# Three of five pieces of the inner layer norms: from VectorE to ScalarE and GpSimd

## The chip, the cores and the metric

The kernel runs on one core of a Trainium2 chip. The metric is the device time of one execution in microseconds (us). The core has these engines, each with an instruction queue of its own that is served in order: TensorE (PE, matmuls and transposes; PEld is its loading of weights), VectorE (DVE), ScalarE (ACT), GpSimd (POOL) and SyncE (SP), which here only issues DMA transfers. An engine waits at an instruction until the semaphores for it have come; whatever stands behind that instruction waits too.

## The reference

Two layers, each with a token mixer and a feed-forward part, both followed by a layer norm of the sum with the input. SEQ is 256, D_MODEL 2048, all in float32.

```python
for li in range(DEPTH):                              # DEPTH = 2
    proj = x @ w_in[li]
    ...                                              # three groups of heads
    mix = jnp.concatenate([ya, yb, yc], axis=-1) @ w_out[li]
    x = layer_norm(DEEPNORM_ALPHA * x + mix, ln1_g[li], ln1_b[li])
    ffn = (jax.nn.silu(x @ w_gate[li]) * (x @ w_up[li])) @ w_down[li]
    x = layer_norm(DEEPNORM_ALPHA * x + ffn, ln2_g[li], ln2_b[li])

def layer_norm(x, g, b, eps=1e-5):
    mu = xf.mean(-1, keepdims=True)
    var = jnp.mean(jnp.square(xf - mu), -1, keepdims=True)
    return (xf - mu) * lax.rsqrt(var + eps) * g + b
```

## The kernel before, in words

The 256 tokens are two tiles of 128 rows, t = 0 and 1; each lies in SBUF as `xs[t]`, 128 x 2048 (in rows of the order, `x0_75` and `x1_76`). All large products go through `run_groups`: a group is a block of up to 1024 output columns, and a step is one k (128 rows of the weights) for one t. The weights come in pairs of steps by DMA from SyncE's queue (`raw`, three buffers). `convert` splits each 128x1024 weight tile: ScalarE rounds it to `whi` (line 226), VectorE subtracts that from it to give `wlo` (line 227), and there are six buffers of each. A step then is six matmuls, two blocks of 512 columns in three passes on line 283: hi by hi, lo by hi, hi by lo. The left side is x transposed: TensorE transposes 128x128 blocks of x into a PSUM tile `aux` (line 306), and `split` writes the rounded half with ScalarE (`xth`, line 296) and the rest with VectorE (`xtl`, line 297). `pump(n)` asks for the conversions up to step n: it is called ahead of each step, so that the order in which the engines get their instructions is that of the program's text, sorted by a scheduler that also weighs priorities.

A layer norm stands between two groups. `res_evac` adds a finished block to x on VectorE (line 326) and takes its statistics (`bst`, line 330). `ln_finish` joins them (`mv`, `ve`) and GpSimd raises the variance to the power -1/2 (`rs`, line 342). `ln_apply` then norms x in five pieces, PIECES = (0,2), (2,4), (4,8), (8,12), (12,16) in blocks of 128 columns; a piece takes two operations of VectorE: (x - mean)*g on line 350 and *rs + b on line 353. They are here called p0 to p4. Between the two operations of t=1's first piece `between` pumps one weight conversion. Four norms are made: three inner ones (after out-projection 0 at 428 us of the span, after feed-forward 0 at 1152, after out-projection 1 at 1577) and the final one, which writes the output.

The first group behind an inner norm is skewed (`skew_in` 4): it takes k0 to k3 for t=0, then k0 to k3 for t=1, then from k4 on both t of each k. `xt_hooks` says where in this row the pieces are normed (`apply`) and transposed (`need`); `after(k, t)` runs behind each step. p2, the first far piece, is needed from k4 on, p3 from k8, p4 from k12. Behind the norm, VectorE holds the conversions of k4 and on.

Of the kernel before, what the change touches and what calls it, by code (L numbers as in the profile page):

```python
# [1 line left out]

# [1 line left out]

# [6 lines left out]
F32 = mybir.dt.float32  # L11
F32R = mybir.dt.float32r
BF16 = mybir.dt.bfloat16
AF = mybir.ActivationFunctionType
ALU = mybir.AluOpType
AX = mybir.AxisListType

P = 128
# [118 lines left out]
class Trunk:  # L137
# [79 lines left out]
    def convert(self, j):  # L217
        nc = self.nc
        w = self.steps[j][0]["width"]
        raw = self.raws[j // 2]  # L220
        src = raw[:, j % 2, 0:w]
        hi = self.wp.tile([P, 1024], F32R, name="whi", tag="whi", bufs=H_BUFS)
        lo = self.wp.tile([P, 1024], F32R, name="wlo", tag="wlo", bufs=H_BUFS)
        for o in range(0, w, w // 2 if j == 0 else w):
            s = slice(o, o + (w // 2 if j == 0 else w))
            nc.scalar.copy(out=hi[:, s], in_=src[:, s])  # L226
            nc.vector.tensor_tensor(out=lo[:, s], in0=src[:, s], in1=hi[:, s].bitcast(F32), op=ALU.subtract)  # L227
        self.whl[j] = (hi, lo)
        self.whl.pop(j - H_BUFS, None)
        if j % 2 == 1:  # L230
            del self.raws[j // 2]
            self.load_pair(j // 2 + RAW_BUFS)

    def pump(self, upto):

        while self.done < min(upto, len(self.steps)):
            self.convert(self.done)
            self.done += 1

    def run_groups(self, groups):  # L240

        nc = self.nc
        self.steps, self.pairs, self.raws, self.whl = [], [], {}, {}
        for g in groups:
            g["base"] = len(self.steps)
            for k in range(g["nk"]):
                self.steps.append((g, k))
                if k % 2 == 0:
                    self.pairs.append(g["src"](k))
        for p in range(RAW_BUFS):  # L250
            self.load_pair(p)
            for c in {1: (1,), 2: (2, 3)}.get(p, ()):
                for t in range(NT):
                    self.load_x(nc.sync, t, c)
        self.done = 0
        for g in groups:
            nk, nb, si, so = g["nk"], len(g["blocks"]), g.get("skew_in", 1), g.get("skew_out", 1)
            allb = tuple(range(nb))
            order = [(k, t, allb) for t in range(NT) for k in range(si)]
            order += [(k, t, allb) for k in range(si, nk - so) for t in range(NT)]  # L260
            order += [(k, t, (b,)) for t in range(NT) for b in allb for k in range(nk - so, nk)]
            banks = {}
            g["start"]()
            for (k, t, bs) in order:
                j = g["base"] + k
                if (k, t, bs[-1]) == (nk - 1, NT - 1, nb - 1) and "mid" in g:
                    g["mid"]()
                xh, xl = g["lhs"](k, t)
                ahead = AHEAD if k >= nk - so or k < si else FAR_AHEAD
                if k < si and t == 0 and si > 1:  # L270
                    self.pump(g["base"] + si)
                elif so > 1 and k == nk - 1 and t == NT - 1:
                    self.pump(j + SKEW + 1)
                else:
                    self.pump(j + ahead + 1)
                hi, lo = self.whl[j]
                for b in bs:
                    if (t, b) not in banks:
                        banks[t, b] = self.psum.tile([P, 512], F32, name="mm", tag="mm", bufs=MM_BUFS)
                for i, (lt, wt) in enumerate(((xh, hi), (xh, lo), (xl, hi))):  # L280
                    for b in bs:
                        o, w = g["blocks"][b]
                        nc.tensor.matmul(banks[t, b][:, 0:w], lt, wt[:, o:o + w],  # L283
                                         start=(k == 0 and i == 0), stop=(k == nk - 1 and i == 2))
                g["progress"] = k + 1
                if k == nk - 1:
                    for b in bs:
                        g["evac"](t, b, banks[t, b])
                if "after" in g and bs[-1] == nb - 1:
                    g["after"](k, t)  # L290
                if bs[-1] == nb - 1:
                    self.tasks.tick(g.get("budget", BUDGET) * g["width"] / 1024)


    def split(self, ps, hi, lo):
        self.nc.scalar.copy(out=hi, in_=ps)  # L296
        self.nc.vector.tensor_tensor(out=lo, in0=ps, in1=hi.bitcast(F32), op=ALU.subtract)  # L297

    def new_xt(self):
        return [self.xtp.tile([P, 4, SEQ], F32R, name=n, tag=n, bufs=4) for n in ("xth", "xtl")]  # L300
# [34 lines left out]
    def ln_finish(self, t, stats):  # L335
        nc = self.nc
        mv = self.small.tile([P, 2], F32, name="mv")
        nc.vector.bn_aggr(out=mv, in_=stats[t].rearrange("p c s -> p (c s)"))
        ve = self.small.tile([P, 1], F32, name="ve")
        nc.vector.tensor_scalar(out=ve, in0=mv[:, 1:2], scalar1=1e-5, scalar2=None, op0=ALU.add)  # L340
        rs = self.small.tile([P, 1], F32, name="rs")
        nc.gpsimd.tensor_tensor(out=rs, in0=ve, in1=self.mhalf[:, 0:1], op=ALU.pow)  # L342
        return mv, rs

    def ln_apply(self, t, k0, k1, mv, rs, between):
        nc = self.nc
        s = slice(k0 * P, k1 * P)
        z = self.xs[t][:, s]
        lg, lb = self.ln
        nc.vector.scalar_tensor_tensor(out=z, in0=z, scalar=mv[:, 0:1], in1=lg[:, s], op0=ALU.subtract, op1=ALU.mult)  # L350
        if between is not None:
            between()
        nc.vector.scalar_tensor_tensor(out=z, in0=z, scalar=rs, in1=lb[:, s], op0=ALU.mult, op1=ALU.add)  # L353

    def xt_hooks(self, mvrs):

        xt = self.xt = [None] * 4
        applied, done = set(), set()
        piece = lambda k: next(i for i, (a, b) in enumerate(PIECES) if a <= k < b)

        def apply(t, i, between=None):
            if (t, i) not in applied:
                applied.add((t, i))
                if mvrs is not None:
                    self.ln_apply(t, *PIECES[i], *mvrs[t], between)

        def need(t, i):
            if (t, i) not in done:
                done.add((t, i))
                apply(t, i)  # L370
                a, b = PIECES[i]
                if xt[a // 4] is None:
                    xt[a // 4] = self.new_xt()
                x = self.xs[t]
                self.tr_block([x[:, k * P:(k + 1) * P] for k in range(a, b)], xt[a // 4], a % 4, t)
                if i == 0:
                    apply(t, 1)

        def lhs(k, t):
            need(t, piece(k))  # L380
            hi, lo = xt[k // 4]
            s = slice(t * P, (t + 1) * P)
            return hi[:, k % 4, s], lo[:, k % 4, s]

        def after(k, t):
            if k == 0:
                need(t, 1)
            for i, (a, b) in enumerate(PIECES):
                if i >= 2 and (k, t) == (a - 4, 1):
                    apply(0, i)  # L390
                if i >= 2 and (k, t) == (a - 3, 1):
                    apply(1, i)
                if i >= 2 and (k, t) == (a - 2, 1):
                    need(0, i)
                if i >= 2 and (k, t) == (a - 1, 0):
                    need(1, i)
        return dict(lhs=lhs, after=after, apply=apply, need=need)

# [659 lines left out]
                groups[-1].update(skew_out=SKEW, mid=lambda: self.hooks["need"](0, 0))  # L1058
        return groups

    def ln_ready(self, t, stats):
        if t == 0:
            self.mvrs = {}
            self.hooks = self.xt_hooks(self.mvrs)
        self.mvrs[t] = self.ln_finish(t, stats)
        self.hooks["apply"](t, 0, (lambda: self.pump(self.done + 1)) if t else None)

    def ffn_groups(self, l):
        groups = []
        box = {}  # L1070
        for hf in range(2):
# [27 lines left out]
            for gi in range(2):  # L1099
# [15 lines left out]
                def evac(t, b, bank, hf=hf, gi=gi, last=last):  # L1115
                    self.res_evac(t, 2 * gi + b, bank, hf == 0, box["stats"] if hf else None)
                    if last and b == 1:
                        self.ln_ready(t, box["stats"])
                        if l == DEPTH - 1:
                            for i, (k0, k1) in enumerate(PIECES):  # L1120
                                self.hooks["apply"](t, i)
                                s = slice(k0 * P, k1 * P)
                                self.nc.sync.dma_start(out=self.out[0, t * P:(t + 1) * P, s], in_=self.xs[t][:, s])

# [53 lines left out]
```

## Time and profile before

| | |
|---|---|
| median of 3 runs | 2317.28 us (2317.12 to 2317.84) |
| the profiled execution, its own time | 2317.24 us |
| its span, first to last instruction | 2315.5 us |
| TensorE busy | 2296.5 us |
| VectorE busy | 1564.7 us |
| ScalarE busy | 1027.3 us |
| GpSimd busy | 36.7 us |
| granted TensorE clock, mean | 0.998 |

The span starts with the first instruction and ends with the last; 1.74 us of the execution's time lie around it. A busy time is the union of an engine's instructions. Where TensorE, the busiest, stands idle, time is lost; idle time of the others costs something only where it reaches TensorE.

### The profile page before, as it was taken

What the parts mean: (1) busy time and instruction counts of PE and PEld (TensorE: products, weight loads), DVE (VectorE), ACT (ScalarE), POOL (GpSimd) and SP (SyncE); (2) the same over time, 40 slices, a digit from 0 to 9 for tenths busy, and PEclk for the clock granted to TensorE, in tenths of its full rate; (3) what the DMA queues carried; (4) which work ended last, traced back from release to release, by engine and by line L of the source; (5) the groups of instructions that cost most, each with busy time, mean ns of one, the idle gap of its engine ahead of it and who ended that gap; (6) DMA issues with size and microseconds to landing.
All of it is one profiled execution on the core that took longest, in us unless ns stands there. A gap on an engine that the chain in (4) does not pass through costs nothing.

```text
span 2315.5 us, 27648 instructions
## 1 busy us (share of the span) xinstructions
PE 2296.5 (99%) x10474; PEld 1899.5 (82%) x10474; DVE 1564.7 (68%) x2596; ACT 1027.3 (44%) x1289; POOL 36.7 (2%) x78
## 2 busy tenths in 40 slices
PE   9999999999999999999999999999999999999997
PEld 7888888788888888888888888887888888888886
DVE  5885575767766447766578756657776764576765
ACT  5645554444444334444345465534444433444432
POOL 0000100000000000000000010000000000000000
PEclk9999999999999999999999999999999999999999
DMA  8555455555555555555556544565556555556553
GB/s 281 189 207 172 149 182 200 195 205 184 202 197 195 188 198 182 198 202 190 177 182 207 193 163 147 182 210 208 184 191 207 183 200 198 182 188 212 182 197 112
DMA packets 178934, 441.16 MB, mean 191 GB/s; under 512 B 15120, under 2 KB 22256, under 8 KB 177776
## 3 DMA queue, kind: packets, MB, share of 16 engines
q1 hardware_dynamic: 178656, 439.32, 55.7%
q8 instruction: 82, 1.34, 0.2%
q14 instruction: 52, 0.43, 0.1%
q10 hardware_dynamic: 144, 0.07, 0.0%
HBM read 437.25 MB, written 2.10 MB: 190 GB/s over the span
## 4 chain that ended last, share of the span: by engine, by line
PE 97%; DVE 2%; issue 1%; DMA 0%; ACT 0%; SPq 0%; POOLq 0%; POOL 0%
PE mm L283 94%; PE aux L306 1%; DVE x L353 0%; PE aux L573 0%; PE aux L668 0%; DVE x L350 0%; PE aux L435 0%; PE aux L758 0%; DVE bst L330 0%; DMA raw<-w_in 0%; PE aux L798 0%; PE aux L691 0%; PE aux L546 0%; DVE wlo L227 0%; ACT xth L296 0%
## 5 line engine op out<-in xcount | busy, mean ns | idle before, releaser
L227 DVE TENSOR_TENSOR wlo<-raw,whi 128x1024 fp32r<-128x1024 f32 (+2 forms) x817 | 983.1, 1212 | 659.1 <-ACT whi L226 653.6
L226 ACT CAST whi<-raw 128x1024 fp32r<-128x1024 f32 (+2 forms) x817 | 851.9, 1045 | 1138.5 <-PE mm L283 1100.6
L283 PE MATMUL mm<-whi,xth 128*128 128x512 f32 (+1 forms) x2560 | 808.6, 391 | 2.5 <-ACT xth L296 2.2
L283 PE MATMUL mm<-wlo,xth 128*128 128x512 f32 (+1 forms) x2560 | 798.4, 387 | 0.0
L283 PE MATMUL mm<-whi,xtl 128*128 128x512 f32 (+1 forms) x2560 | 796.9, 387 | 0.0
L283 PEld LDWEIGHTS mm<-wlo,xth 128*128 128x128 f32 x2560 | 476.6, 188 | 98.3 <-DVE wlo L227 0.2
L283 PEld LDWEIGHTS mm<-whi,xtl 128*128 128x128 f32 x2560 | 476.3, 188 | 98.6
L283 PEld LDWEIGHTS mm<-whi,xth 128*128 128x128 f32 x2560 | 469.9, 188 | 98.4 <-ACT xth L296 4.5
L283 PE MATMUL mm<-whi,gth 128*128 128x512 f32 x704 | 222.0, 389 | 0.0
L283 PE MATMUL mm<-whi,gtl 128*128 128x512 f32 x704 | 222.0, 389 | 0.0
L283 PE MATMUL mm<-wlo,gth 128*128 128x512 f32 x704 | 221.9, 389 | 0.0
L422 DVE STREAM_TRANSPOSE gtr<-sil 32x128 f32<-32x128 f32 x704 | 213.0, 303 | 11.2
L283 PEld LDWEIGHTS mm<-whi,gth 128*128 128x128 f32 x704 | 132.2, 188 | 27.6
L283 PEld LDWEIGHTS mm<-whi,gtl 128*128 128x128 f32 x704 | 132.2, 188 | 27.4
L283 PEld LDWEIGHTS mm<-wlo,gth 128*128 128x128 f32 x704 | 132.2, 188 | 27.3
L422 DVE STREAM_TRANSPOSE qk<-stg 32x128 f32<-32x128 f32 x256 | 77.4, 302 | 4.2
L296 ACT CAST xth<-aux 128x512 fp32r<-128x512 f32 (+1 forms) x58 | 29.1, 512 | 35.7 <-PE aux L306 29.9
L297 DVE TENSOR_TENSOR xtl<-aux,xth 128x512 fp32r<-128x512 f32 (+1 forms) x58 | 33.8, 594 | 6.8 <-ACT xth L296 6.8
L342 POOL TENSOR_TENSOR rs<-ve,mhalf 128x1 f32<-128x1 f32 x8 | 5.7, 718 | 1743.1 <-DVE ve L340 1743.1
L1140 DVE TENSOR_TENSOR gtl<-gtr,gth 128x512 fp32r<-128x512 f32 x44 | 29.9, 680 | 0.7
L1087 ACT ACTIVATE sil<-mm 128x512 f32<-128x512 f32 x44 | 25.9, 594 | 9.9 <-PE mm L283 9.9
L1090 DVE TENSOR_TENSOR sil<-mm,sil 128x512 f32<-128x512 f32 x44 | 28.2, 683 | 1.4 <-ACT sil L1087 1.4
(156 smaller groups left out, 635.6 us busy)
## 6 DMA issues: line engine op xcount, KB each, us to landing
raw<-w_gate SPq DMA_DIRECT2D x176, 512.0 KB, 3.7
raw<-w_up SPq DMA_DIRECT2D x176, 512.0 KB, 4.6
raw<-w_down SPq DMA_DIRECT2D x88, 1024.0 KB, 5.1
raw<-w_in SPq DMA_DIRECT2D x78, 1024.0 KB, 4.8
raw<-w_out SPq DMA_DIRECT2D x32, 1024.0 KB, 5.2
raw<-w_in SPq DMA_DIRECT2D x52, 512.0 KB, 4.0
raw<-w_in SPq DMA_DIRECT2D x16, 256.0 KB, 4.0
lng<-ln_g SPq DMA_DIRECT2D x4, 1024.0 KB, 7.7
```

The source lines that it names most:

```text
L226: nc.scalar.copy(out=hi[:, s], in_=src[:, s])
L227: nc.vector.tensor_tensor(out=lo[:, s], in0=src[:, s], in1=hi[:, s].bitcast(F32), op=ALU.subtract)
L283: nc.tensor.matmul(banks[t, b][:, 0:w], lt, wt[:, o:o + w], start=(k == 0 and i == 0), stop=(k == nk - 1 and i == 2))
L296: self.nc.scalar.copy(out=hi, in_=ps)
L297: self.nc.vector.tensor_tensor(out=lo, in0=ps, in1=hi.bitcast(F32), op=ALU.subtract)
L306: self.nc.tensor.transpose(out=ps[:, i * P:(i + 1) * P], in_=s, identity=self.ident)
L342: nc.gpsimd.tensor_tensor(out=rs, in0=ve, in1=self.mhalf[:, 0:1], op=ALU.pow)
L422: self.nc.vector.transpose(out=out[32 * j:32 * j + 32, 0:n, 32 * i:32 * i + 32], in_=in_[32 * i:32 * i + 32, 0:n, 32 * j:32 * j + 32])
L1087: nc.scalar.activation(out=box["s", t], in_=bank, func=AF.Silu)
L1090: nc.vector.tensor_tensor(out=g, in0=bank, in1=g, op=ALU.mult)
L1140: nc.vector.tensor_tensor(out=lo, in0=gt, in1=hi.bitcast(F32), op=ALU.subtract)
```

## The change

In the three inner norms the pieces p2 to p4 go to other engines. `ln_finish` has two more operations of GpSimd for nm = -mean*rs. `ln_apply_far` makes a piece by one ScalarE activation (x*rs + nm, in place) and two GpSimd operations of 128x512, times g and plus b. `ln_apply` keeps p0 and p1 on VectorE without anything between its two operations; one conversion is asked for behind the second. The hooks move: p2 of t=0 is asked for in `ln_ready`, p2 of t=1 behind the first step of t=1, p3 and p4 of both t six and five steps ahead of their use and behind the last far piece. While the skew lasts, VectorE's half of a conversion is tied behind the last `xtl` (`fence`). The transposes of p2 of t=1 move from behind k3 of t=0, that is from ahead of all of t=1's steps, to behind k3 of t=1; those of p3 and p4 of t=1 stand directly behind those of t=0. The final norm keeps all pieces on VectorE (`far=False`).

```diff
@@ convert
-            nc.vector.tensor_tensor(out=lo[:, s], in0=src[:, s], in1=hi[:, s].bitcast(F32), op=ALU.subtract)
+            with ExitStack() as st:
+                if self.fence is not None:
+                    st.enter_context(self.tc.issue_after(self.fence))
+                nc.vector.tensor_tensor(out=lo[:, s], in0=src[:, s], in1=hi[:, s].bitcast(F32), op=ALU.subtract)
...
-    def pump(self, upto):
+    def pump(self, upto, behind=None):
+        self.fence = behind
...
-                    self.pump(j + ahead + 1)
+                    self.pump(j + ahead + 1, self.last_lo if 1 < si and k < si else None)
@@ ln_finish
+        nm = self.small.tile([P, 1], F32, name="nm")
+        nc.gpsimd.tensor_tensor(out=nm, in0=mv[:, 0:1], in1=rs, op=ALU.mult)
+        nc.gpsimd.tensor_scalar(out=nm, in0=nm, scalar1=-1.0, scalar2=0.0, op0=ALU.mult, op1=ALU.add)
...
+    def ln_apply_far(self, t, k0, k1, mv, rs, nm):
+        nc = self.nc
+        s = slice(k0 * P, k1 * P)
+        z = self.xs[t][:, s]
+        lg, lb = self.ln
+        nc.scalar.activation(out=z, in_=z, func=AF.Identity, bias=nm, scale=rs)
+        nc.gpsimd.tensor_tensor(out=z, in0=z, in1=lg[:, s], op=ALU.mult)
+        self.last_far = nc.gpsimd.tensor_tensor(out=z, in0=z, in1=lb[:, s], op=ALU.add).ins
...
-        if between is not None:
-            between()
-        nc.vector.scalar_tensor_tensor(out=z, in0=z, scalar=rs, in1=lb[:, s], op0=ALU.mult, op1=ALU.add)
+        last = nc.vector.scalar_tensor_tensor(out=z, in0=z, scalar=rs, in1=lb[:, s], op0=ALU.mult, op1=ALU.add).ins
+        if behind is not None:
+            behind(last)
@@ xt_hooks, after(k, t)
             if k == 0:
+                if mvrs is not None and t:
+                    with self.tc.issue_after(self.last_hi):
+                        apply(1, 2)
                 need(t, 1)
             for i, (a, b) in enumerate(PIECES):
-                if i >= 2 and (k, t) == (a - 4, 1):
-                    apply(0, i)
-                if i >= 2 and (k, t) == (a - 3, 1):
-                    apply(1, i)
-                if i >= 2 and (k, t) == (a - 2, 1):
+                if i < 2:
+                    continue
+                near = i == 2
+                skewed = near and mvrs is not None
+                if mvrs is not None and i > 2:
+                    for u in range(NT):
+                        if (k, t) == (a - 6 + u, 1):
+                            with self.tc.issue_after(self.last_far), self.tc.issue_after(self.last_hi):
+                                apply(u, i)
+                if (k, t) == (a - 2, 1):
                     need(0, i)
-                if i >= 2 and (k, t) == (a - 1, 0):
+                if (k, t) == ((a - 1, 1) if skewed else (a - 1, 0) if near else (a - 2, 1)):
                     need(1, i)
@@ ln_ready
-        self.hooks["apply"](t, 0, (lambda: self.pump(self.done + 1)) if t else None)
+        self.hooks["apply"](t, 0, (lambda ins: self.pump(self.done + 1, ins)) if t else None)
+        if not final and t == 0:
+            self.hooks["apply"](t, 2)
```

Where instructions stand is shown at the first inner norm. `whi_3629` before and `whi_3635` after is the conversion of k2; the next is k3, then k4, k5 and so on. First ScalarE, from the conversion of k2 on, before:

```order
L226 CAST whi_3629<-raw_3520 128x1024
L226 CAST whi_3665<-raw_3520 128x1024
L296 CAST xth_3644<-aux_3646 128x2x128
L226 CAST whi_3746<-raw_3555 128x1024
L226 CAST whi_3763<-raw_3555 128x1024
L296 CAST xth_3644<-aux_3684 128x2x128
```

and after:

```order
L227 CAST whi_3635<-raw_3520 128x1024
L361 ACTIVATE x0_75<-x0_75,nm_3621,rs_3619 128x512
L227 CAST whi_3675<-raw_3520 128x1024
L303 CAST xth_3650<-aux_3652 128x2x128
L227 CAST whi_3745<-raw_3555 128x1024
L227 CAST whi_3767<-raw_3555 128x1024
L303 CAST xth_3650<-aux_3693 128x2x128
L303 CAST xth_3650<-aux_3716 128x2x128
```

The activation of t=0's p2 now stands ahead of the conversion of k3 and of the first `xth` (p0 of t=0, out of `aux_3652`), the one of t=1 behind the `xth` of t=1's p0 (`aux_3716`).

Next VectorE behind the norm's last operation on t=1's p1. Before, with the `xtl` of t=1's p2 (`aux_3711`), p0 (`aux_3718`) and p1 (`aux_3733`), the conversions of k4 to k8 (`wlo_3747` to `wlo_3788`), and the `xtl` of t=0's p2 (`aux_3756`):

```order
L297 TENSOR_TENSOR xtl_3710<-aux_3711,xth_3709 128x4x128
L297 TENSOR_TENSOR xtl_3645<-aux_3718,xth_3644 128x2x128
L227 TENSOR_TENSOR wlo_3747<-raw_3555,whi_3746 128x1024
L297 TENSOR_TENSOR xtl_3645<-aux_3733,xth_3644 128x2x128
L227 TENSOR_TENSOR wlo_3764<-raw_3555,whi_3763 128x1024
L227 TENSOR_TENSOR wlo_3777<-raw_3596,whi_3776 128x1024
L227 TENSOR_TENSOR wlo_3781<-raw_3596,whi_3780 128x1024
L227 TENSOR_TENSOR wlo_3788<-raw_3669,whi_3787 128x1024
L297 TENSOR_TENSOR xtl_3710<-aux_3756,xth_3709 128x4x128
```

After, from the joined statistics of t=1 on; `wlo_3676` is the conversion of k3, `aux_3716` and `aux_3734` are p0 and p1 of t=1, `aux_3757` p2 of t=0 and `aux_3780` p2 of t=1:

```order
L345 BN_AGGR mv_3664<-bst_2937 128x2
L347 TENSOR_SCALAR ve_3666<-mv_3664 128x1
L370 SCALAR_TENSOR_TENSOR x1_76<-x1_76,mv_3664,lng_3349 128x256 x2
L371 SCALAR_TENSOR_TENSOR x1_76<-x1_76,rs_3668,lnb_3350 128x256
L231 TENSOR_TENSOR wlo_3676<-raw_3520,whi_3675 128x1024
L371 SCALAR_TENSOR_TENSOR x1_76<-x1_76,rs_3668,lnb_3350 128x256
L304 TENSOR_TENSOR xtl_3651<-aux_3716,xth_3650 128x2x128
L304 TENSOR_TENSOR xtl_3651<-aux_3734,xth_3650 128x2x128
L231 TENSOR_TENSOR wlo_3746<-raw_3555,whi_3745 128x1024
L304 TENSOR_TENSOR xtl_3756<-aux_3757,xth_3755 128x4x128
L231 TENSOR_TENSOR wlo_3768<-raw_3555,whi_3767 128x1024
L231 TENSOR_TENSOR wlo_3791<-raw_3596,whi_3790 128x1024
L304 TENSOR_TENSOR xtl_3756<-aux_3780,xth_3755 128x4x128
```

The conversion of k3, which before stood ahead of the last statistics of t=1, now stands between the second operations of t=1's near pieces. The `xtl` of p2 of t=0 moves from behind the conversion of k8 to behind that of k4; that of t=1, which stood ahead of all of them, moves behind those of k5 and k6 (`wlo_3768`, `wlo_3791`).

Last GpSimd after; before, its queue held only the two `rs` here:

```order
L352 TENSOR_SCALAR nm_3621<-nm_3621 128x1
L362 TENSOR_TENSOR x0_75<-x0_75,lng_3349 128x512
L363 TENSOR_TENSOR x0_75<-x0_75,lnb_3350 128x512
L349 TENSOR_TENSOR rs_3668<-ve_3666,mhalf_90 128x1
L351 TENSOR_TENSOR nm_3670<-mv_3664,rs_3668 128x1
L352 TENSOR_SCALAR nm_3670<-nm_3670 128x1
L362 TENSOR_TENSOR x1_76<-x1_76,lng_3349 128x512
L363 TENSOR_TENSOR x1_76<-x1_76,lnb_3350 128x512
L362 TENSOR_TENSOR x0_75<-x0_75,lng_3349 128x512
L363 TENSOR_TENSOR x0_75<-x0_75,lnb_3350 128x512
L362 TENSOR_TENSOR x1_76<-x1_76,lng_3349 128x512
L363 TENSOR_TENSOR x1_76<-x1_76,lnb_3350 128x512
```

GpSimd's `rs` of t=1 stands behind both operations on p2 of t=0; the far pieces stand in one row behind it, each waiting for its activation. SyncE's load of the next norm's g (line 318, its buffer being the g of this one) now waits for the last of these products instead of for VectorE; it keeps its place among the weight loads.

## Rows read from the trace of the kernel before

**Rows 1.** The page: busy time, share of the span and instructions of each engine.

```profile
PE 2296.5 (99%) x10474; PEld 1899.5 (82%) x10474; DVE 1564.7 (68%) x2596; ACT 1027.3 (44%) x1289; POOL 36.7 (2%) x78
```

**Rows 2.** What TensorE waited for: total us, times, longest us.

```profile
PE mm L283 <- ACT xth L296: 2.2, 3, 0.7
PE aux L306 <- DVE x L353: 1.7, 3, 0.6
```

**Rows 3.** Timeline of TensorE, norm one: start, duration, line, what, count, idle before.

```profile
430.66 0.65 PE L283 MATMUL mm<-whi,xth 128*128 128x512 f32 x2
...
437.13 0.84 PE L306 MATMUL aux<-cst_sb,x 128*128 128x128 f32 x6 [0.57 <-DVE x L353]
438.71 0.73 PE L283 MATMUL mm<-whi,xth 128*128 128x512 f32 x2 [0.73 <-ACT xth L296]
...
445.00 0.68 PE L283 MATMUL mm<-whi,xth 128*128 128x512 f32 x2
...
447.81 0.62 PE L283 MATMUL mm<-whi,xth 128*128 128x512 f32 x2
...
449.17 0.62 PE L283 MATMUL mm<-whi,xth 128*128 128x512 f32 x2
```

**Rows 4.** Timeline of VectorE in the same stretch, same columns.

```profile
431.90 1.22 DVE L227 TENSOR_TENSOR wlo<-raw,whi 128x1024 fp32r<-128x1024 f32 x1
...
433.96 0.25 DVE L338 BATCH_NORM_AGGREGATE mv<-bst 128x2 f32<-128x24 f32 x1
...
435.85 1.14 DVE L353 SCALAR_TENSOR_TENSOR x<-x,rs,lnb 128x256 f32<-128x256 f32 x2
...
437.30 1.14 DVE L353 SCALAR_TENSOR_TENSOR x<-x,rs,lnb 128x512 f32<-128x512 f32 x2
```

**Rows 5.** Timeline of ScalarE in the same stretch, same columns.

```profile
429.00 1.05 ACT L226 CAST whi<-raw 128x1024 fp32r<-128x1024 f32 x1 [5.75 <-PE mm L283]
430.16 0.37 ACT L296 CAST xth<-aux 128x256 fp32r<-128x256 f32 x1
```

**Rows 6.** Timeline of GpSimd in the same stretch, same columns.

```profile
428.26 0.72 POOL L342 TENSOR_TENSOR rs<-ve,mhalf 128x1 f32<-128x1 f32 x1 [146.45 <-DVE ve L340]
434.95 0.72 POOL L342 TENSOR_TENSOR rs<-ve,mhalf 128x1 f32<-128x1 f32 x1 [5.97 <-DVE ve L340]
```

**Rows 7.** A group of GpSimd by shape: count, busy us, mean ns, idle before.

```profile
L626 POOL TENSOR_TENSOR rrs<-rrs,dm 128x4 f32<-128x4 f32 x4 | 0.8, 202 | 0.3
```

**Rows 8.** One line each: ns minimum, median, maximum, first and last start, forms.

```profile
L652 POOL TENSOR_TENSOR mixc<-mixc,nrm x16: 592/599/1585, 232.5 to 1386.2; 128x192 f32<-128x192 f32 x16
L350 DVE SCALAR_TENSOR_TENSOR x<-x,mv,lng x40: 469/742/751, 428.1 to 2310.2; 128x512 f32<-128x512 f32 x24, 128x256 f32<-128x256 f32 x16
```

**Rows 9.** The page's group of the activations of 128x512.

```profile
L1087 ACT ACTIVATE sil<-mm 128x512 f32<-128x512 f32 x44 | 25.9, 594 | 9.9 <-PE mm L283 9.9
```

**Rows 10.** Timeline of GpSimd at 1384, two of its products.

```profile
1383.58 2.14 POOL L652 TENSOR_TENSOR mixc<-mixc,nrm 128x192 f32<-128x192 f32 x2
```

**Rows 11.** Timeline of VectorE in the same stretch.

```profile
1384.02 1.25 DVE L227 TENSOR_TENSOR wlo<-raw,whi 128x1024 fp32r<-128x1024 f32 x1 [5.33 <-ACT whi L226]
```

**Rows 12.** Timeline of VectorE at 203.

```profile
203.00 1.22 DVE L227 TENSOR_TENSOR wlo<-raw,whi 128x1024 fp32r<-128x1024 f32 x1 [1.84 <-ACT whi L226]
```

**Rows 13.** Timeline of GpSimd: the small scalings at 203 and 238.

```profile
203.75 0.52 POOL L623 TENSOR_SCALAR rve<-ssa 128x2 f32<-128x2 f32 x1 [5.51 <-ACT work L803]
...
238.06 0.19 POOL L623 TENSOR_SCALAR rve<-ssa 128x2 f32<-128x2 f32 x1
```

**Rows 14.** The second half: us, busy us of each engine (x instructions), clock, DMA, GB/s.

```profile
445.00:468.00 23.00, 23.00 (x110) 19.09 (x110) 17.87 (x21) 10.44 (x12) 0.00 (x0) 1.00 0.91 327
```

**Rows 15.** SyncE's DMA queue around the second half.

```profile
454.44 0.34 SPq L318 DMA_DIRECT2D lng<-ln_g  x1
459.45 0.37 SPq L214 DMA_DIRECT2D raw<-w_gate  x1
```

**Rows 16.** The page's DMA issues: count, KB each, median us to landing.

```profile
raw<-w_gate SPq DMA_DIRECT2D x176, 512.0 KB, 3.7
```

More of the change, by code (lines that the diff above doesn't have):

```diff
@@ L1 @@
 import math
+from contextlib import ExitStack
 import numpy as np
@@ L238, in pump @@
             self.done += 1
+        self.fence = None
     def run_groups(self, groups):
@@ L295, in split @@
     def split(self, ps, hi, lo):
-        self.nc.scalar.copy(out=hi, in_=ps)
-        self.nc.vector.tensor_tensor(out=lo, in0=ps, in1=hi.bitcast(F32), op=ALU.subtract)
+        self.last_hi = self.nc.scalar.copy(out=hi, in_=ps).ins
+        self.last_lo = self.nc.vector.tensor_tensor(out=lo, in0=ps, in1=hi.bitcast(F32), op=ALU.subtract).ins
     def new_xt(self):
@@ L342, in ln_finish, with ln_apply @@
         nc.gpsimd.tensor_tensor(out=rs, in0=ve, in1=self.mhalf[:, 0:1], op=ALU.pow)
-        return mv, rs
-    def ln_apply(self, t, k0, k1, mv, rs, between):
+        nm = self.small.tile([P, 1], F32, name="nm")
+        nc.gpsimd.tensor_tensor(out=nm, in0=mv[:, 0:1], in1=rs, op=ALU.mult)
+        nc.gpsimd.tensor_scalar(out=nm, in0=nm, scalar1=-1.0, scalar2=0.0, op0=ALU.mult, op1=ALU.add)
+        return mv, rs, nm
+    def ln_apply_far(self, t, k0, k1, mv, rs, nm):
[6 more added lines that the diff above has]
+        self.last_far = nc.gpsimd.tensor_tensor(out=z, in0=z, in1=lb[:, s], op=ALU.add).ins
+    def ln_apply(self, t, k0, k1, mv, rs, nm, behind):
         nc = self.nc
@@ L359, in xt_hooks, with apply @@
         piece = lambda k: next(i for i, (a, b) in enumerate(PIECES) if a <= k < b)
-        def apply(t, i, between=None):
+        def apply(t, i, behind=None, far=None):
             if (t, i) not in applied:
                 applied.add((t, i))
-                if mvrs is not None:
-                    self.ln_apply(t, *PIECES[i], *mvrs[t], between)
+                if mvrs is not None and (i >= 2 if far is None else far):
+                    self.ln_apply_far(t, *PIECES[i], *mvrs[t])
+                elif mvrs is not None:
+                    self.ln_apply(t, *PIECES[i], *mvrs[t], behind)
         def need(t, i):
@@ L1059, in out_groups, with ln_ready @@
         return groups
-    def ln_ready(self, t, stats):
+    def ln_ready(self, t, stats, final=False):
         if t == 0:
@@ L1117, in evac @@
                     if last and b == 1:
-                        self.ln_ready(t, box["stats"])
+                        self.ln_ready(t, box["stats"], l == DEPTH - 1)
                         if l == DEPTH - 1:
                             for i, (k0, k1) in enumerate(PIECES):
-                                self.hooks["apply"](t, i)
+                                self.hooks["apply"](t, i, far=False)
                                 s = slice(k0 * P, k1 * P)
```

## The prediction

> **What bounds the kernel now.** I read the page's busy times first: TensorE is busy 99% of the span [rows 1], so only time in which it stands idle, or gets more to do, counts. The view of its waits comes second: two waits belong to the inner norms, three times each, 2.2 us for ScalarE's `xth` and 1.7 us for VectorE's line 353 [rows 2]. The timeline of norm one shows where. TensorE is through with t=0's four steps at 436.56 and waits 0.57 us for the second operation on p2 of t=1, whose transposes stand ahead of all of t=1's steps; the `xth` behind these six transposes costs another 0.73 us [rows 3]. VectorE's timeline has the cause: a conversion of 1.22 us at 431.90 stands in front of the joined statistics at 433.96, and at 435.85 and 437.30 operations on far pieces stand between those that t=1's first step needs [rows 4]. The other norms have the same pair. From 445.00 to 468.00 TensorE never stops, with VectorE busy 17.87 of 23 us [rows 14]. So the change can win at most the 3.9 us of these waits, 0.17% of the time; 0.2% is about what this measurement tells from no change.
>
> **What goes and what comes.** Each inner norm loses 12 VectorE operations of 0.742 us [rows 8], 8.9 us, and gains 6 activations, 12 GpSimd products of 128x512 and 4 tiny GpSimd operations. Where VectorE's 8.9 us stood beside TensorE's work they bring nothing; the two waits are all that they cost.
>
> An activation of 128x512 takes 0.594 us [rows 9]; the one shown reads PSUM, mine reads SBUF, and I take 0.59. A GpSimd product of 128x512 is in no row. From below: 128x4 takes 0.202 us [rows 7] and 128x192 0.592 at least [rows 8], which is 2.07 ns an element, hence 0.592 + 320 x 0.00207 = 1.26 us. From above, in proportion: 0.592 x 512/192 = 1.58. I take 1.3, because the small row shows that a part of the time does not grow with the size. Both operations on a piece are then 2.6 to 3.2 us instead of 1.5 on VectorE.
>
> The Trainium skill (GPSIMD Engine Reference, the table that reconciles measured numbers) gives 4497 ns for 2048 elements against 2293 on VectorE; an estimate by a quarter would be 1.12 us, a little under my lower end, and the sum below would hardly move. No row here has that size.
>
> *Start of the skew, norm one.* GpSimd ends `rs` at 428.98 [rows 6]; two tiny operations of 0.2 us each and the handing over let the activation of t=0's p2 start at about 429.65. It stands ahead of k3's conversion on ScalarE, which ran at 429.00, and that stands ahead of the first `xth`, which ran at 430.16 [rows 5]. Now: activation to 430.2, conversion 430.1 to 431.1, `xth` at 431.08. So TensorE's first step of t=0 starts at 431.58 instead of 430.66 [rows 3]: 0.92 us later.
>
> *End of t=0.* TensorE's work up to 436.56 took 5.90 us; it now has to wait for VectorE's half of k3's conversion, which has moved behind t=1's first second operation. With `xth` late the `xtl` in front of the joined statistics is late too, and 433.96 becomes 434.15; `rs` of t=1 then runs 434.65 to 435.37 (0.72 as before), the norm's second operation on p0 starts at 435.55, and the conversion runs from 435.94 to 437.16. TensorE can use it at 437.25, some 0.5 to 0.7 us after it wants it, and with two passes of 0.45 us (a third of the step of 1.36, 447.81 to 449.17) t=1 begins at 438.16. Before it began at 438.71 [rows 3].
>
> *t=1.* From there to k4 it took 6.29 us [rows 3]; four transposes of p2 come in, about 0.3 us, so k4 starts near 444.75 instead of 445.00. Up to here the two waits, 1.3 us, have shrunk to a gain of 0.25 us, since ScalarE's place and k3's conversion take their room: three norms 0.75 us.
>
> *From k4 on.* VectorE now has the `xtl` of t=1's p2 behind the conversions of k5 and k6. By my schedule these run at 444.91 and 446.04, and the `xtl` ends at 447.9; TensorE wants it at 447.9. There is no slack. In this moment, about 444.85, GpSimd begins with p3 of t=0. Does a GpSimd product hold up a VectorE conversion? The trace has the other direction: a scaling of 0.19 us by itself at 238.06 [rows 13] takes 0.52 at 203.75, begun under a conversion from 203.00 to 204.22 [rows 12], and ends just behind it; six such overlaps of six look so. At 1383.58 two products take 2.14 us [rows 10] instead of twice 0.592 [rows 8], with a conversion from 1384.02 [rows 11]. That conversion began before the product under way was through, and took 1.25 instead of 1.22; so from this one row the price for VectorE lies anywhere between nothing and the rest of a product.
>
> The bounds: nothing, if VectorE is never held; one product of 1.2 to 1.35 us, if the first conversion gets in ahead of GpSimd and the product between the two conversions holds the second; two products, 2.5 us, if GpSimd gets in first. I take the middle, 1.2, as both begin within 0.06 us of each other, and the row at 1384 shows a conversion little delayed when it starts upon a running product. Per norm: -0.25 + 1.2 = +0.95.
>
> The Trainium skill (SBUF — State Buffer, who interferes with whom) says that a VectorE instruction with two SBUF inputs and a GpSimd instruction that reads SBUF exclude each other, and that the second to start is fully blocked. The six overlaps agree in one direction; the 1.25 us at 1384.02 neither shows nor refutes the other. By this rule the price would be the 1.2 to 2.5 us just bounded.
>
> **The sum**, against the profiled run's own 2317.24 (0.04 under the median): 2317.24 + 3 x 0.95 = 2320.1, said as 2320.0.
>
> **The rivals.**
>
> *A: both waits simply go.* If ScalarE's and VectorE's new places cost nothing (nm earlier than I think, k3's conversion in time) and GpSimd holds nobody up: 2317.24 - 3.9 = 2313.3. Against it: the order on ScalarE and VectorE is fixed, and the two delays follow from durations in rows. Chance 0.10, and in about half of it some more small gaps around the transposes go too and it passes 0.2%.
>
> *C: no hold-up of VectorE.* Start and skew as worked out, nothing behind: 2317.24 - 0.75 = 2316.5. For it: the conversion at 1384.02. Chance 0.27.
>
> *B, the forecast:* 2320 to 2324, the upper end with 2.5 us in each norm. Chance 0.42, about two thirds of it below 2321.9.
>
> *D, the slower side: GpSimd starves and p3 comes late.* Four products on p3 (5.1 to 6.3 us) must lie between 444.85 and 452.7, where their transposes are wanted. VectorE has six conversions to make there, some 7 us of work at up to 1.22 each. If it goes from one to the next without letting GpSimd in, the products begin only at about 451.8 and end at 457 or later, over 4 us late; with 4.8 as a price: 2316.5 + 3 x 4.8 = 2330.9. It decides from the point at which fewer than three products get in before 450. Against it: VectorE must wait for ScalarE's half of most conversions, since these wait for a buffer that TensorE frees. Chance 0.16.
>
> *E: the weight loads come late.* The load of the next norm's g, at 454.44 before, now waits for GpSimd's last product with g, at about 462 to 464, and the weight load of 459.45 [rows 15] stands behind it. That load has two pairs of steps, 2 x 5.44 us, less its landing of 3.7 [rows 16] and some 0.9 for the issues, before its first conversion: 6.3 us of slack. It costs from 465.7 on, one for one, in the two norms ahead of a feed-forward part; with the last product at 468, 2316.5 + 2 x 2.3 = 2321.1. Chance 0.05.
>
> **How the numbers follow.** Faster by over 0.2% (under 2312.65) is half of A, 0.06 with rounding up. Slower by over 0.2% (over 2321.9) is a third of B, D and a little of E: 0.35. The rest, 0.59, is within 0.2%. The range leaves out half of A below and most of D above: 2313 to 2329. Cases of both signs inside the 0.2% make up the most; the likeliest one's own range is 2320 to 2324.
>
> **What would show it.** ScalarE's first `xth` at about 431.1 and TensorE's first step at 431.6; TensorE waiting for `wlo` of line 231 in k3 of t=0, and no longer for line 371 (353 before); GpSimd's products taking 1.2 to 1.6 us alone, and some with the length of a conversion on top; conversions of more than 1.3 us on VectorE, if it is held; TensorE's wait for `xtl` of line 304 at about 448. The prediction is wrong if conversions stay at 1.22 us while products run (then C), if the waits for lines 313 or 304 behind p3 are of several us (D), or if the products are not within 1.2 to 1.6.

## The result and the profile after

The changed kernel takes 2334.34 us (median of 4 runs, 2334.24 to 2335.13) against 2317.31 of before: a ratio of 1.0075 with a 95% interval of 1.0063 to 1.0087, slower by 17.0 us. The forecast was 2320.0, at most 2329. The range missed, and the profile says at once that something stands in it that the forecast never spoke of.

TensorE's waits, as total, times and longest, are what the forecast talked about, and they are small:

```profile
PE mm L289 <- ACT xth L303: 2.7, 3, 0.9
PE mm L289 <- DVE xtl L304: 2.0, 3, 0.7
PE mm L289 <- DVE wlo L231: 1.6, 3, 0.6
...
PE aux L313 <- DVE x L371: 0.7, 3, 0.3
```

7.0 us where there were 3.9 [rows 2]. But the page has TensorE busy 14.7 us longer [rows 1], with the same 10474 instructions:

```profile
PE 2311.2 (99%) x10474; PEld 1900.3 (81%) x10474; DVE 1563.3 (67%) x2560; ACT 1037.1 (44%) x1307; POOL 107.7 (5%) x130
...
L289 PE MATMUL mm<-whi,gth 128*128 128x512 f32 x704 | 226.2, 395 | 0.0
L289 PE MATMUL mm<-wlo,gth 128*128 128x512 f32 x704 | 226.0, 395 | 0.0
L289 PE MATMUL mm<-whi,gtl 128*128 128x512 f32 x704 | 225.9, 395 | 0.0
```

These three groups are the down-projections, whose left side is `gth` or `gtl`. No line of the change touches them. Before, their rows on the page were:

```profile
L283 PE MATMUL mm<-whi,gth 128*128 128x512 f32 x704 | 222.0, 389 | 0.0
L283 PE MATMUL mm<-whi,gtl 128*128 128x512 f32 x704 | 222.0, 389 | 0.0
L283 PE MATMUL mm<-wlo,gth 128*128 128x512 f32 x704 | 221.9, 389 | 0.0
```

12.2 us more in these 2112 matmuls (226.2 + 226.0 + 225.9 against 222.0 + 221.9 + 222.0). The timeline of TensorE shows that it is no wait but the pace. In each pair below five matmuls start between the first row's start and the last row's. Before:

```profile
739.79 0.39 PE L283 MATMUL mm<-whi,gth 128*128 128x512 f32 x1
...
740.92 0.39 PE L283 MATMUL mm<-whi,gth 128*128 128x512 f32 x1
```

and after:

```profile
739.71 0.40 PE L289 MATMUL mm<-whi,gth 128*128 128x512 f32 x1
...
740.87 0.39 PE L289 MATMUL mm<-whi,gth 128*128 128x512 f32 x1
```

1.13 us against 1.16, so 0.226 and 0.232 us apart, evenly all the way (0.2267 and 0.2323 where more of them are taken, as the expectations below do); the granted clock is 1.00 in both. Put side by side in order of their starts, matmul by matmul, the changed kernel loses 1.8, 1.8 and 1.7 us at the three norms and about 3 us in each of the four halves of the down-projections.

At norm one the timelines can be read against the forecast. TensorE:

```profile
431.62 0.73 PE L289 MATMUL mm<-whi,xth 128*128 128x512 f32 x2 [0.90 <-ACT xth L303]
...
433.51 0.41 PE L313 MATMUL aux<-cst_sb,x 128*128 128x128 f32 x2 [0.25 <-DVE x L371]
...
437.90 0.73 PE L289 MATMUL mm<-wlo,xth 128*128 128x512 f32 x2 [0.54 <-DVE wlo L231]
...
445.54 0.71 PE L289 MATMUL mm<-whi,xth 128*128 128x512 f32 x2
...
449.85 1.19 PE L289 MATMUL mm<-whi,xtl 128*128 128x512 f32 x4 [0.66 <-DVE xtl L304]
```

ScalarE:

```profile
429.54 0.82 ACT L361 ACTIVATE x<-x,nm,rs 128x512 f32<-128x512 f32 x1 [6.40 <-POOL nm L352]
430.26 1.03 ACT L227 CAST whi<-raw 128x1024 fp32r<-128x1024 f32 x1
431.20 0.36 ACT L303 CAST xth<-aux 128x256 fp32r<-128x256 f32 x1
```

VectorE:

```profile
431.94 1.43 DVE L371 SCALAR_TENSOR_TENSOR x<-x,rs,lnb 128x256 f32<-128x256 f32 x1
...
436.64 1.21 DVE L231 TENSOR_TENSOR wlo<-raw,whi 128x1024 fp32r<-128x1024 f32 x1
...
445.75 3.44 DVE L231 TENSOR_TENSOR wlo<-raw,whi 128x1024 fp32r<-128x1024 f32 x2
449.12 0.68 DVE L304 TENSOR_TENSOR xtl<-aux,xth 128x512 fp32r<-128x512 f32 x1
449.72 8.43 DVE L231 TENSOR_TENSOR wlo<-raw,whi 128x1024 fp32r<-128x1024 f32 x5
```

GpSimd:

```profile
430.44 1.27 POOL L362 TENSOR_TENSOR x<-x,lng 128x512 f32<-128x512 f32 x1 [0.93 <-ACT x L361]
431.79 1.29 POOL L363 TENSOR_TENSOR x<-x,lnb 128x512 f32<-128x512 f32 x1
...
445.90 2.21 POOL L362 TENSOR_TENSOR x<-x,lng 128x512 f32<-128x512 f32 x1 [4.67 <-ACT x L361]
448.19 2.13 POOL L363 TENSOR_TENSOR x<-x,lnb 128x512 f32<-128x512 f32 x1
450.29 2.27 POOL L362 TENSOR_TENSOR x<-x,lng 128x512 f32<-128x512 f32 x1
```

The activation at 429.54 stands ahead of k3's conversion at 430.26 (429.00 before), and the first `xth` comes at 431.20 instead of 430.16 [rows 5]; TensorE starts t=0 at 431.62 (forecast: 431.58). GpSimd's product from 431.79 to 433.08 holds line 371 on t=0's p1 (0.48 alone): 431.94, 1.43 us. The later links of t=1's chain come 0.65 to 0.8 us later than forecast, up to k3's conversion at 436.64 and TensorE's pass on it at 437.90. From 445.75 products and conversions take turns: two conversions in 3.44 us, five in 8.43, and products of 2.1 to 2.3 us instead of 1.29 alone.

### The profile page after: what moved, and what is told of

Same layout as the page of the kernel before. It is cut to its first block, busy times and chain, and to the rows that moved or that the text cites. A ratio compares the mean times of both kernels' runs of the same rounds, so it can differ in the third digit from the quotient of the medians.

```text
span 2332.7 us, 27708 instructions
## 1 busy us (share of the span) xinstructions
PE 2311.2 (99%) x10474; PEld 1900.3 (81%) x10474; DVE 1563.3 (67%) x2560; ACT 1037.1 (44%) x1307; POOL 107.7 (5%) x130
## 3 DMA queue, kind: packets, MB, share of 16 engines
HBM read 437.25 MB, written 2.10 MB: 188 GB/s over the span
## 4 chain that ended last, share of the span: by engine, by line
PE 97%; DVE 2%; issue 0%; POOL 0%; DMA 0%; ACT 0%; SPq 0%; ACTq 0%; POOLq 0%
PE mm L289 93%; PE aux L313 1%; DVE x L371 0%; DVE wlo L231 0%; PE aux L603 0%; PE aux L698 0%; PE aux L465 0%; PE aux L788 0%; DVE bst L337 0%; DMA raw<-w_in 0%; POOL rs L349 0%; PE aux L828 0%; DVE xtl L304 0%; ACT whi L227 0%; DVE x L370 0%
## 5 line engine op out<-in xcount | busy, mean ns | idle before, releaser
L231 DVE TENSOR_TENSOR wlo<-raw,whi 128x1024 fp32r<-128x1024 f32 (+2 forms) x817 | 1001.9, 1236 | 658.7 <-ACT whi L227 653.6
L289 PE MATMUL mm<-whi,gth 128*128 128x512 f32 x704 | 226.2, 395 | 0.0
L289 PE MATMUL mm<-wlo,gth 128*128 128x512 f32 x704 | 226.0, 395 | 0.0
L289 PE MATMUL mm<-whi,gtl 128*128 128x512 f32 x704 | 225.9, 395 | 0.0
L362 POOL TENSOR_TENSOR x<-x,lng 128x512 f32<-128x512 f32 x18 | 33.4, 1857 | 29.1 <-ACT x L361 29.1
L363 POOL TENSOR_TENSOR x<-x,lnb 128x512 f32<-128x512 f32 x18 | 32.9, 1826 | 1.4
```

Of the source, the lines that this page charges most:

```text
L289: nc.tensor.matmul(banks[t, b][:, 0:w], lt, wt[:, o:o + w], start=(k == 0 and i == 0), stop=(k == nk - 1 and i == 2))
L362: nc.gpsimd.tensor_tensor(out=z, in0=z, in1=lg[:, s], op=ALU.mult)
L363: self.last_far = nc.gpsimd.tensor_tensor(out=z, in0=z, in1=lb[:, s], op=ALU.add).ins
```

## The experiments

### Where the down-projections' 12 us come from

`nm` is a new tile of the pool `small`, in four buffers of 32 bytes a partition. In the built program the tiles of the attention and of the feed-forward part, which are allocated behind it, lie 128 bytes further, `gth` at 149664 instead of 149536 in each partition; the weight tiles `whi` and `wlo` (the first at 98336) and the left sides `xth` and `xtl` (the first at 40992) lie ahead of it and stay. In the kernel before all these left sides and weight tiles lie multiples of 512 bytes apart. The tile `gpad` ahead of `gth` (G_PAD = 32 words) is never written or read. So placement was one theory, and the new instructions or their order the other. Four kernels tell them apart.

Without `gpad`, so that `gth` is back at its old address:

```diff
-                        self.gpool.tile([P, G_PAD], F32, name="gpad")
```

> The changed kernel without the 128-byte tile gpad, so that gth and gtl (the left sides of the down-projections) begin at the same SBUF address as in the kernel before; the four new nm tiles of 32 bytes had moved them by 128 bytes. Theory 1 (placement): the down-projections' matmuls, 0.2323 us apart after against 0.2267 before, go back to 0.2267; 12.0 us of the 17.0 lost come back, near 2322.3. Theory 2 (the new instructions or their order slow the down-projections): it stays near 2334.

Measured: 2322.19 (2321.84 to 2323.19), ratio 1.0023 (1.0013 to 1.0032). 12.15 us came back.

The other way round, the kernel before with nothing changed but the size of that unused tile:

```diff
-G_PAD = 32
+G_PAD = 64
```

> The kernel before with gpad of 256 bytes instead of 128: gth and gtl 128 bytes further, where the changed kernel has them; the instructions are the same ones. Theory 1 (placement): near 2329.3, with 0.2323 us between matmuls in the down-projections alone. Theory 2: 2317.3, as before.

Measured: 2329.51, ratio 1.0053 (1.0038 to 1.0068): 12.4 us slower without a new instruction. Theory 2 has fallen.

All tiles that the large products read, moved by the same 128 bytes:

```diff
         self.xtp = pool("xtp")
+        self.xtp.tile([P, 32], F32, name="xpad")
```

> The kernel before with a pad of 128 bytes ahead of all xth, xtl, raw, whi, wlo, gth and gtl: all move together. Theory 1a (the distance between the left side and the weight tiles counts): 2317.3. Theory 1b (the left side's own address counts): every large matmul at 0.2323 apart, about 2.5 per cent of some 2200 us, near 2370. Theory 2: 2317.3.

Measured: 2316.91, ratio 0.9999 (0.9990 to 1.0008). It isn't the address of the left side by itself.

```diff
-G_PAD = 32
+G_PAD = 160
```

> The kernel before with gpad of 640 bytes instead of 128: gth and gtl 512 bytes further. Theory 1 with a period of 512 bytes or a divisor of it that is not 128: 2317.3. Theory 1 with any other dependence on the address (a boundary that is crossed, a longer period): something else, up to 2329.3. Theory 2: 2317.3.

Measured: 2317.14, ratio 1.0000 (0.9991 to 1.0010). 512 bytes cost nothing.

Three more kernels ask what the distance is between, and what its period is. The pad now stands behind `xth` and `xtl` and ahead of the weight tiles:

```diff
         self.wp = pool("wp")
+        self.wp.tile([P, 32], F32, name="wpad")
```

> The kernel before with a pad of 128 bytes ahead of raw, whi, wlo, gth and gtl; xth and xtl stay. Now the down-projections' left sides keep their distance to the weight tiles, and those of all other products lose it. Theory 1a (distance between left side and weight tiles): the 7680 matmuls with xth and xtl slow to 0.2323 us apart, 7680 x 0.0056 = 43 us, near 2360, and the down-projections stay at 0.2267. Rival (the left side's distance to something else, such as x or the constants): 2329.3, as with gth shifted alone.

Measured: 2357.91, ratio 1.0176 (1.0161 to 1.0192), 40.8 us slower. The page's rows have changed sides: the groups with `xth` on the left are slow, those with `gth` are not. First the row of the kernel before, then two of this one:

```profile
L283 PE MATMUL mm<-whi,xth 128*128 128x512 f32 (+1 forms) x2560 | 808.6, 391 | 2.5 <-ACT xth L296 2.2
```

```profile
L284 PE MATMUL mm<-whi,xth 128*128 128x512 f32 (+1 forms) x2560 | 822.1, 396 | 2.5 <-ACT xth L297 2.2
...
L284 PE MATMUL mm<-whi,gth 128*128 128x512 f32 x704 | 222.0, 389 | 0.0
```

Distances of 64 and 256 bytes, again by `gpad` alone:

```diff
-G_PAD = 32
+G_PAD = 48      # before_pad48; 96 in before_pad96
```

> The kernel before with gth and gtl 64 bytes further. If any distance that is no multiple of 512 bytes costs the same: 2329.5. If the cost grows with the distance: between 2317.3 and 2329.5.

> The kernel before with gth and gtl 256 bytes further. If the period is 256 bytes: 2317.3. If it is 512: 2329.5 or another value above 2317.3.

Measured: 2330.85 with 64 bytes, ratio 1.0059 (1.0044 to 1.0074), and 2317.15 with 256, ratio 1.0000 (0.9990 to 1.0010). Moving the left side against the weight tiles by 256 or 512 bytes is free; 64 and 128 bytes cost 13.7 and 12.4 us over 2112 matmuls, 6.5 and 5.9 ns each. The weights as loaded (`raw`) moved together with `whi` and `wlo` in every run, so the runs do not tell these apart; of these three the matmuls read only `whi` and `wlo`. Why the chip does so no run here shows.

### Where the norms' 5 us come from

What is left of the loss without `gpad` is 2322.19 - 2317.14 = 5.05 us, 1.7 a norm. Matmul by matmul it is lost at the norms, 1.8, 1.7 and 1.7 us. The attention, whose tiles are still 128 bytes further there, loses nothing: up to the first norm the matmuls keep to their places within 0.07 us, and in the second layer's attention too. Three edits on that kernel and one on the kernel before look at the norms; the kernel before took 2317.27 beside them.

The activation of t=0's p2 moved behind the first `xth`:

```diff
@@ need
                 if i == 0:
                     apply(t, 1)
+                    if t == 0 and mvrs is not None:
+                        with self.tc.issue_after(self.last_hi):
+                            apply(0, 2)
@@ ln_ready
-        if not final and t == 0:
-            self.hooks["apply"](t, 2)
```

> The changed kernel without gpad (2322.2), with one more edit: the activation of t=0's p2 is asked for behind the first xth instead of ahead of k3's conversion. Theory 1 (ScalarE's order costs what TensorE waits there): the wait of 0.90 us for the first xth goes in each of three norms, and that of 0.25 for line 371 behind it; 2319 to 2319.5. Theory 2 (VectorE's chain of t=1 with k3's conversion sets the time anyway): the gain comes back as a longer wait for k3's wlo, 2321 to 2322.

Measured: 2317.77, ratio 1.0002 (0.9993 to 1.0010): 4.4 us better, more than theory 1 gave. So the run does not price ScalarE's place alone: other orders changed with it, which the edit doesn't say. On VectorE the `xtl` of t=1's p2 stands behind one conversion instead of two, and TensorE's wait for it is gone as well; the first operation on t=1's p1 stands behind k3's conversion; and t=1's p1 is transposed directly behind its p0. VectorE is still held there: line 370 takes 1.17 us at 433.16, 0.47 alone. Of TensorE's waits in the norms these remain:

```profile
PE aux L313 <- POOL x L363: 1.8, 3, 0.6
PE mm L289 <- DVE wlo L231: 1.3, 3, 0.5
```

To that, the conversion of k3 back to its old place ahead of t=1's joined statistics:

```diff
@@ ln_ready
+        if t:
+            self.pump(self.done + 1)
         self.mvrs[t] = self.ln_finish(t, stats)
-        self.hooks["apply"](t, 0, (lambda ins: self.pump(self.done + 1, ins)) if t else None)
+        self.hooks["apply"](t, 0)
```

> As the one before, and the conversion of k3 is asked for ahead of t=1's joined statistics, where it stood in the kernel before. Theory 1: the wait of 0.54 us for k3's wlo goes too, 1.6 us over three norms, near 2317.5. Theory 2 (t=1's chain is then 1.1 us later and TensorE waits for its transposes instead): no gain over the run before.

Measured: 2315.76, ratio 0.9993 (0.9984 to 1.0001): 2.0 us better again, about the 1.6 of theory 1; t=1's chain does not come late. One wait is left, 0.6 us in each norm, and it is GpSimd's, at the transposes of p3:

```profile
453.11 0.66 PE L313 MATMUL aux<-cst_sb,x 128*128 128x128 f32 x4 [0.62 <-POOL x L363]
```

GpSimd's products, shortened to 16 of 512 columns in the kernel without `gpad` (the far pieces then lack most of g and b):

```diff
-        nc.gpsimd.tensor_tensor(out=z, in0=z, in1=lg[:, s], op=ALU.mult)
-        self.last_far = nc.gpsimd.tensor_tensor(out=z, in0=z, in1=lb[:, s], op=ALU.add).ins
+        nc.gpsimd.tensor_tensor(out=z[:, 0:16], in0=z[:, 0:16], in1=lg[:, s][:, 0:16], op=ALU.mult)
+        self.last_far = nc.gpsimd.tensor_tensor(out=z[:, 0:16], in0=z[:, 0:16], in1=lb[:, s][:, 0:16], op=ALU.add).ins
```

> The changed kernel without gpad, whose GpSimd products cover 16 of 512 columns (the rest of g and b is left out in the far pieces); order and waits are the same. Theory 1 (products hold up VectorE's conversions): conversions behind k4 back to 1.22 us, the waits of 0.66 us for xtl and 0.25 for line 371 go in each norm, 2322.2 - 2.7 = 2319.5. Theory 2 (the xtl is late through its place behind two conversions alone): the wait at k4 stays, 2321.5 to 2322.

Measured: 2317.31, ratio 0.9999 (0.9990 to 1.0008): 4.9 us better, with the same order on the engines, and more than the 2.7 of theory 1. The line of all conversions, with minimum, median and maximum in ns, is in the changed kernel

```profile
L231 DVE TENSOR_TENSOR wlo<-raw,whi x817: 683/1225/2348, 6.4 to 2305.3; 128x1024 fp32r<-128x1024 f32 x156, 128x776 fp32r<-128x776 f32 x7, 128x512 fp32r<-128x512 f32 x1
```

and with short products

```profile
L231 DVE TENSOR_TENSOR wlo<-raw,whi x817: 681/1224/1254, 6.5 to 2288.5; 128x1024 fp32r<-128x1024 f32 x156, 128x776 fp32r<-128x776 f32 x7, 128x512 fp32r<-128x512 f32 x1
```

so no conversion is held any more; the longest took 2.35 us before that. GpSimd's own rows show the other direction: a product of 0.22 us by itself takes over 1 us when it meets the conversions.

```profile
445.26 1.15 POOL L362 TENSOR_TENSOR x<-x,lng 128x16 f32<-128x16 f32 x1 [6.64 <-ACT x L361]
...
447.53 0.22 POOL L362 TENSOR_TENSOR x<-x,lng 128x16 f32<-128x16 f32 x1
```

```profile
445.11 2.37 DVE L231 TENSOR_TENSOR wlo<-raw,whi 128x1024 fp32r<-128x1024 f32 x2
447.41 0.68 DVE L304 TENSOR_TENSOR xtl<-aux,xth 128x512 fp32r<-128x512 f32 x1
```

And the links of the forecast that its own sum had without any hold-up come out within 0.03 us, TensorE's start of t=0 at 431.61 (forecast 431.58) and its pass on k3's conversion at 437.26 (437.25):

```profile
431.61 0.73 PE L289 MATMUL mm<-whi,xth 128*128 128x512 f32 x2 [0.90 <-ACT xth L303]
...
437.26 0.73 PE L289 MATMUL mm<-wlo,xth 128*128 128x512 f32 x2 [0.35 <-DVE wlo L231]
```

Two of TensorE's waits in the norms stay in this run, 3.8 us in all:

```profile
PE mm L289 <- ACT xth L303: 2.7, 3, 0.9
...
PE mm L289 <- DVE wlo L231: 1.1, 3, 0.4
```

They are ScalarE's new place and k3's conversion. So with the hold-ups of VectorE gone, the changed order just equals the kernel before, 2317.31 against 2317.27. The next run has neither wait and is 3.7 us faster than the kernel before.

Last the kernel before, with one condition changed. The transposes of t=1's p2 come behind k3 of t=1, as in the change, but the pieces all stay on VectorE:

```diff
@@ xt_hooks, after(k, t)
-                if i >= 2 and (k, t) == (a - 1, 0):
+                if i >= 2 and (k, t) == ((a - 1, 1) if i == 2 and mvrs is not None else (a - 1, 0)):
                     need(1, i)
```

> The kernel before with one edit: in the inner norms the transposes of t=1's p2 come behind k3 of t=1 instead of ahead of t=1's steps; nothing goes to ScalarE or GpSimd. Theory 1 (the two waits of before come from this place, not from VectorE's load): both waits go, 3.9 us, near 2313.4. Theory 2 (VectorE has too much work there, so that the wait only moves to the xtl of p2 at k4): 2316 to 2319.

Measured: 2313.61 (2313.42 to 2314.52), ratio 0.9985 (0.9976 to 0.9994), 3.7 us faster than before and 20.7 faster than the change. TensorE's waits in the whole span:

```profile
PE aux L173 <- DVE mhalf L175: 1.2, 1, 1.2
PE aux L306 <- DMA x<-x: 1.1, 1, 1.1
PE mm L283 <- ACT whi L226: 0.2, 1, 0.2
```

Both waits of [rows 2] are gone. In norm one t=1 begins at 437.17 instead of 438.71 [rows 3]:

```profile
436.33 0.75 PE L306 MATMUL aux<-cst_sb,x 128*128 128x128 f32 x4
437.17 0.73 PE L283 MATMUL mm<-whi,xth 128*128 128x512 f32 x2
```

VectorE's two operations on t=1's p2 now stand behind the near pieces, around a conversion, and the `xtl` comes in time for k4:

```profile
437.86 0.74 DVE L350 SCALAR_TENSOR_TENSOR x<-x,mv,lng 128x512 f32<-128x512 f32 x1
...
439.66 0.75 DVE L353 SCALAR_TENSOR_TENSOR x<-x,rs,lnb 128x512 f32<-128x512 f32 x1
...
445.46 0.68 DVE L297 TENSOR_TENSOR xtl<-aux,xth 128x512 fp32r<-128x512 f32 x1
```

## Why the prediction was wrong

**The failed step is the first one**, that "only time in which it stands idle, or gets more to do, counts". TensorE got nothing more to do and took 12 us longer, since the same matmuls ran at another pace. The change's `nm` had been priced as four tiny operations of GpSimd; its 128 bytes of SBUF had not been priced at all. G_PAD, an unused tile in front of `gth`, stood in the code and was not asked about. Shown in both directions: 12.15 us back without the pad, 12.4 us lost by the pad alone.

**The norms' term was mis-sized**: +0.95 us each forecast, 1.7 measured (5.05/3). Up to k4 the sum had a gain of 0.25 us; matmul by matmul there is a loss of 0.65, and 0.03 with short products. By its parts:

- *Start of the skew*, +0.92: 431.62 against 431.58. Right, with luck in it: the activation took 0.82 us instead of 0.59, so that k3's conversion began 0.72 us behind its start and not 0.45, but the norm began 0.10 us earlier than before and TensorE started 0.42 us behind the `xth` instead of 0.50. The wait of 0.90 us has the size of the forecast delay.
- *End of t=0*, 437.25: 437.90. The order and the wait for k3's conversion were right in kind; the size (0.54 us, forecast 0.5 to 0.7) was met only with the hold-up, and is 0.35 without it. The first pair of products was taken to hold nobody, and it held line 371 by about 0.95 us, of the 1.14 that the product still had to run. TensorE then waits for line 371 too, 0.25 us, which the forecast had excluded. With short products the link is at 437.26. Here the sum asked for hold-ups only from k4 on, although the products of p2 run in the middle of VectorE's chain.
- *k4*, 444.75: 445.54, the same 0.7 us, and a little more: the pass behind the wait takes 0.57 us (437.90 to 438.47), not 0.45.
- *From k4 on*, +1.2: right in size and in kind. From k4 to the end of the norm the changed kernel loses another 1.2 us, of which TensorE's wait for the `xtl` shows 0.66; with short products it loses 0.1 there.
- *Products of 1.26 to 1.58 us, taken as 1.3*: 1.27 to 1.29 alone, up to 2.28 in turns with conversions.

The rule of the Trainium skill (SBUF — State Buffer, who interferes with whom), that a VectorE instruction with two SBUF inputs and a GpSimd instruction that reads SBUF exclude each other, agrees with what the trace now shows in both directions: line 371 at 1.43 us instead of 0.48, conversions up to 2.35 instead of 1.22, products up to 2.28 instead of 1.29. An `xtl`, which takes one input from PSUM, was not held: the one at 449.12 took 0.68 us in the middle of a product of 2.13 from 448.19. The row at 1384 from which a conversion "little delayed" was read [rows 11] was too weak to stand against it.

**The rivals.** A and C are out: the waits did not simply go, and VectorE is held. D is out as well, though the time is near its 2330.9, which is chance. Its sign did come, only two products begin before 450, but not its price: VectorE lets GpSimd in after each conversion, and p3's transposes wait for nobody in the changed kernel, where TensorE is late enough; only when the other delays are taken away does p3 cost 0.6 us a norm. E was not seen: the load of the next g came at 462.93 (forecast 462 to 464) with the weight load behind it at 464.02, before the 465.7 from which it was to cost, and no wait of TensorE in the norms goes back to a weight load. In the chances, 0.35 for slower takes in all of E, though E's own time, 2321.1, lies under 2321.9.

**The bound of the gain** held: at most 3.9 us. The kernel with the moved transposes alone takes 3.7 of them. The waits came from the place of p2's transposes, not from VectorE's load, so no work had to leave VectorE.

## What to carry to other kernels

Before an edit's instructions are priced, look at what its tiles do to the addresses of those behind them: here 128 bytes of a tiny tile cost 12 us, more than all waits together, and an unused pad in the code was the sign. A wait that looks like too much work on an engine may be a question of where its consumer stands; try to move the consumer first. And work moved to GpSimd takes its time out of VectorE's where the VectorE instructions beside it take both inputs from SBUF, as the conversions and line 371 do here.

## What the runs showed that was not expected

In the down-projections matmuls keep their pace of 0.2267 us when their left side is moved against the weight tiles by 256 or 512 bytes; by 128 bytes each takes 0.0059 us longer, by 64 bytes 0.0065 (12.4 and 13.7 us over 2112 matmuls). In the products with `xth` only 128 bytes were tried; they cost 40.8 us over 7680 matmuls, 0.0053 us each.
